# Query parts made a group ahead, own weights split before the seven-product sum, value pages requested before products, in a one-layer hybrid step

## The chip, the cores and the metric

The kernel runs on one core of a Trainium2 chip. Its measure is the device time of one execution in microseconds (us); the time of a kernel is the median of its runs. The engines that matter are TensorE (PE, with PEld for its weight loads), VectorE (DVE), ScalarE (ACT), GpSimd (POOL) and SyncE (SP); the last two also issue transfers.

## The reference: one step of a hybrid decoder

One layer takes 512 new prompt tokens and 8 x 4 sample tokens (each sample has 512 past tokens in four pages of 128 rows), 544 tokens in all, of width 1024. Everything is fp32.

```
def half_ffn(x, g_pre, g_post, w_gate, w_up, w_down):
    h = rmsnorm(x, g_pre)
    u = jax.nn.silu(h @ w_gate) * (h @ w_up)
    return x + 0.5 * rmsnorm(u @ w_down, g_post)
...
logits = jnp.einsum('bqhcd,bkhcd->bchqk', q, k, preferred_element_type=jnp.float32) * (ATT_DQ ** -0.5)
...
p = jax.nn.softmax(logits, axis=-1)
a = p[:, 0] - lam * p[:, 1]
return jnp.einsum('bhqk,bkhd->bqhd', a.astype(v.dtype), v)
```

The layer is a half FFN (inner width 2816), a token mixer, and a second half FFN. The mixer runs two groups of four heads side by side: differential attention (each head has two components of 64 dimensions with a softmax each; the second is subtracted with a factor) and an mLSTM with matrix memory. Samples attend to their cached pages of keys and values and to their own new tokens.

## The kernel before

**Precision and tiling.** Tokens lie along the free dimension in two halves of 272. TensorE multiplies in a rounded fp32 form, and precision is kept by splitting an operand into a high and a low part: `parts` casts a raw weight tile to its high part on ScalarE (L241) and subtracts that from the raw tile on VectorE for the low part (L242). A product is then three matmuls: high x high, high x low, low x high (L253 to L255 for plain products; L489 to L491 for the products of a fast scheme with seven block products, `seven`; L751 to L753 for `plain`, rows of weights that the scheme leaves out and which are called the own rows: `OWN` is 6 rows of 128).

**What sets the order.** The program is written as Python generators that take turns, and a scheduler of the framework then sets the order of the instructions on each engine, under the waits for data and for buffers. Each engine works through its own list in order. Tiles rotate through pools: "acc" and "aux" have three PSUM banks each, "smp" two; an "aux" bank (`ps_tile`) is free again when its last reader is done.

**FFN down products** (`down`, L709 to L833). At the end, four tiles of outputs (i = 0 to 3) are made from the third block product of the scheme: the weights are split (`parted(sums, i)`), `seven` runs its products, a part of the work that finishes the other half is taken (`_take(finish, ...)`: norm and the bridge into the mixer, with the sums "ssp" of squares, L320 and L351, that a product with ones at L285 adds up over the partitions), then the own weights of the tile (128x768) are split and multiplied. Both FFNs use this code.

**The mixer** (lines about 1180 to 1700). The projections of the mixer's input (L253 to L255, with weights split as they come) are interleaved with the attention of the prompt, the mLSTM and the samples, one head after another. For a head, `key_parts` makes the high and low parts of the keys ("cs", L1289 and L1290, 64x512), and `attn_block` handles one block of 128 queries. `query_parts` makes the four parts of the queries: for each component the high part twice (into the component's own 64 partitions and into the other 64, by ScalarE, L1299) and the low part twice (by VectorE, L1301): four casts and four subtractions of 64x128 a block. Their buffer is one tile "vb" of which there is one (`bufs=1`). Two pairs of products, one for a component (L1317), fill one aux bank each; VectorE adds the bias and takes the maximum (L1323, L1325: instructions named CUSTOM_DVE or ISA, that read the bank), ScalarE takes the exponential (L1328), and the parts of the next block are made after the present block's products. Transposes (L1343), the products with the values and the normalisation (L1251, L1252) follow in later turns.

**The samples** (`attn_samples`, L1355 on). Two groups of four samples. Key pages are gathered by POOL's indirect transfers (L1366, seven buffers "pgin"), three ahead, transposed (L1392), copied ("pgT", L1393) and multiplied with the queries. Then for each of four pages, four value pages (one for each sample of the group) are multiplied (L1455), and behind these the four of the next page are requested.

Of the kernel before, what the change touches and what calls it, by code (L numbers as in the profile page):

```python
# [14 lines left out]
ALU = mybir.AluOpType  # L15
# [45 lines left out]
         "q1 m21 t13 h12 d12 q0 q1 m21 t14 h13 d13 q0 q1 m21 t15 h14 d14 q1 m21 t16 h15 d15 q1 t17 h16 d16 q1 "  # L61
         "h17 d17 q1 s01")

NQ = 2
AHEAD = 3
NBK = 32
# [139 lines left out]
class _Builder:  # L206
# [502 lines left out]
    def down(self, li, ns, rows, factors, late, xd, gpost, finish):  # L709
# [30 lines left out]
        def parted(ts, i, n=KH):  # L740
            w = self.w_tiles()
            self.parts(ts[i // 2][:, 0:n, i % 2 * 128:i % 2 * 128 + 128], *(x[:, 0:n] for x in w))
            return w
# [80 lines left out]
        u = raw(2, 0, OWN, None if li else lambda j: self.ha.tile([128, OWN, 256], F32, name="ha"))  # L824
        next(finish)
        for i in range(4):
            w = parted(sums, i)
            ps = self.acc_tile(1)
            self.seven(ps, 3, w, first=True)
            _take(finish, A_STEPS * i // 3 - A_STEPS * max(0, i - 1) // 3)  # L830
            plain(ps, parted(u, i, OWN), 1, 0, OWN, False, True)
            self.post_evac(ps, i, 1, gpost, False, add=True)
        next(finish)  # L833

# [454 lines left out]
            nc.scalar.copy(out=kc[own], in_=k[own, 0:SEQ])  # L1289
            nc.vector.tensor_tensor(out=kc[other], in0=k[own, 0:SEQ], in1=kc[own].bitcast(F32), op=ALU.subtract)  # L1290

    def query_parts(self, q):

        nc = self.nc
        self.qt = qt = self.pg.tile([128, 4, 128], F32R, name="vb", bufs=1)
        for c in range(2):
            own, other = self.comp(c)
            for rows in (own, other):
                nc.scalar.copy(out=qt[rows, c, :], in_=q[own])  # L1299
            for rows in (own, other):  # L1300
                nc.vector.tensor_tensor(out=qt[rows, 2 + c, :], in0=q[own], in1=qt[own, c, :].bitcast(F32),  # L1301
                                        op=ALU.subtract)

    def attn_block(self, h, qb, q, k, vt):
        nc = self.nc
# [1 line left out]
        n = (qb + 1) * 128  # L1307
        if qb == 0:
            self.key_parts(k)
            self.query_parts(q[:, 0:n])  # L1310
            yield
        P = []
        z = wk.tile([128, 6], F32, name="z", bufs=6)
        for c in range(2):
            ps = self.ps_tile()
            for a in range(2):
                nc.tensor.matmul(ps[:, 0:n], lhsT=self.qt[:, 2 * a + c, :], rhs=self.ks[c][:, 0:n],  # L1317
                                 start=a == 0, stop=a == 1)
            L = wk.tile([128, 512], F32, name="L", bufs=5)
            f = max(n - 256, 0)  # L1320
            strip = self.strip[:, h, :]
            if f:
                nc.vector.tensor_tensor_reduce(L[:, 0:f], ps[:, 0:f], strip[:, 0:1].to_broadcast([128, f]), 1.0, -3.0e38,  # L1323
                                               ALU.add, ALU.max, z[:, 4 + c:5 + c])
            nc.vector.tensor_tensor_reduce(L[:, f:n], ps[:, f:n], strip[:, 256 - n + f:256], 1.0,  # L1325
                                           z[:, 4 + c:5 + c] if f else -3.0e38, ALU.add, ALU.max, z[:, c:c + 1])
            nc.vector.tensor_scalar_mul(z[:, c:c + 1], z[:, c:c + 1], -1.0)
            nc.scalar.activation(out=L[:, 0:n], in_=L[:, 0:n], func=AF.Exp, bias=z[:, c:c + 1],  # L1328
                                 accum_out=z[:, 2 + c:3 + c])
            P.append(L)  # L1330
        self.blocks_left -= 1
        if qb < 3:
            self.query_parts(q[:, n:n + 128])
        nc.vector.reciprocal(out=z[:, 2:4], in_=z[:, 2:4])
        nc.vector.tensor_tensor(out=z[:, 3:4], in0=z[:, 3:4], in1=self.nlam, op=ALU.mult)
        nc.vector.tensor_scalar(out=P[1][:, 0:n], in0=P[1][:, 0:n], scalar1=z[:, 3:4], scalar2=None, op0=ALU.mult)
# [22 lines left out]
    def attn_samples(self):  # L1359
# [14 lines left out]
        for g in range(2):  # L1374
# [74 lines left out]
            for j in range(4):  # L1449
                sj = slice(32 * j, 32 * j + 32)  # L1450
                nc.tensor.matmul(po[sj, :], lhsT=an[:, sj], rhs=vtok, start=True, stop=False, tile_position=(0, 32 * j))
            for pg in range(NPG):
                for j in range(4):
                    sj = slice(32 * j, 32 * j + 32)
                    nc.tensor.matmul(po[sj, :], lhsT=aT[:, pg * 128 + 32 * j:pg * 128 + 32 * j + 32], rhs=vps[j],  # L1455
                                     start=False, stop=pg == NPG - 1, tile_position=(0, 32 * j))
                if pg < NPG - 1:
                    vps = [page(1, 4 * g + j, pg + 1) for j in range(4)]
                if g == 0:
                    yield  # L1460
                yield
# [555 lines left out]
```

## Time and profile before

| | us |
|---|---|
| median of three runs | 1106.17 |
| the runs | 1103.99, 1106.17, 1108.48 |
| profiled execution, its own time | 1102.31 |
| span of its profile | 1100.4 |
| TensorE busy / weight loads busy | 1085.4 / 1048.0 |
| VectorE busy / ScalarE busy / POOL busy | 854.4 / 640.4 / 162.8 |

A row of a timeline or of the waits names the line of the program, the engine, the operation and its output and inputs by the program's names. Brackets at a row's end say how long the engine was idle before it, and who ended that. A matmul's record is longer than the distance to the next one's start, because matmuls are pipelined; the distance from start to start is what a matmul costs in a full row. Fused steps of attention (the bias with the maximum) show two rows on VectorE: the operation and a short read of its accumulator.

### The profile page before, as it was taken

How to read it: one execution, taken by the hardware profiler on the slowest of the kernel's cores; microseconds unless marked ns; L12 is line 12 of the kernel's file. 1: busy time of each engine (PE TensorE's matmuls, PEld its weight loads, DVE VectorE, ACT ScalarE, POOL GpSimd, SP SyncE). 2: the span in 40 equal slices, each digit the busy share in tenths (PEclk: the TensorE clock that was granted, in tenths of full speed). 3: DMA queues.
4: the chain of work that ended last, by engine and by line, in shares of the span. 5: the costliest groups of instructions: out<-in, count | busy, mean ns of one | idle time of the engine just before them, and what ended most of it. 6: DMA issues, size and time to landing. Idle time of an engine off the chain costs nothing. (4 is left out here: it accounts for less than half of the span.)

```text
span 1100.4 us, 21550 instructions
## 1 busy us (share of the span) xinstructions
PE 1085.4 (99%) x8610; PEld 1048.0 (95%) x8610; DVE 854.4 (78%) x1630; ACT 640.4 (58%) x1292; POOL 162.8 (15%) x212
## 2 busy tenths in 40 slices
PE   9999999999999999999999999999999999999997
PEld 8999999999999999899889879999999999999997
DVE  5898787887677899658686578799987788957764
ACT  6554554565557757666564557675554455555664
POOL 3100000001110324420244441001000000012000
PEclk9999999999999999999999999999999999999999
DMA  9723233236995245633355646764233323299722
GB/s 265 255 94 116 78 116 115 78 97 188 228 225 170 65 143 155 200 111 87 96 160 172 190 143 189 235 220 135 89 116 94 99 82 102 71 276 208 187 98 82
DMA packets 145620, 160.33 MB, mean 146 GB/s; under 512 B 6045, under 2 KB 135429, under 8 KB 144240
## 3 DMA queue, kind: packets, MB, share of 16 engines
q1 hardware_dynamic: 115040, 99.05, 29.6%
q0 software_dynamic: 27472, 57.14, 21.0%
q10 hardware_dynamic: 3008, 2.78, 0.9%
q8 instruction: 67, 1.10, 0.4%
q14 instruction: 33, 0.27, 0.1%
HBM read 143.19 MB, written 16.28 MB: 145 GB/s over the span
## 5 line engine op out<-in xcount | busy, mean ns | idle before, releaser
L241 ACT CAST wh<-raw 128x512 fp32r<-128x512 f32 (+2 forms) x165 | 127.1, 794 | 98.5 <-PE acc L254 30.3
L242 DVE TENSOR_TENSOR wl<-raw,wh 128x512 fp32r<-128x512 f32 (+2 forms) x165 | 147.2, 904 | 43.2 <-ACT wh L241 42.8
L253 PE MATMUL acc<-h,wh 128*128 128x272 f32 x552 | 164.6, 298 | 0.0
L255 PE MATMUL acc<-h,wl 128*128 128x272 f32 x552 | 160.5, 291 | 0.1
L254 PE MATMUL acc<-h,wh 128*128 128x272 f32 x552 | 159.7, 290 | 0.0
L491 PE MATMUL acc<-t,wl 128*128 128x272 f32 x472 | 136.8, 290 | 0.0
L489 PE MATMUL acc<-t,wh 128*128 128x272 f32 x472 | 136.8, 290 | 0.0
L490 PE MATMUL acc<-t,wh 128*128 128x272 f32 x472 | 136.2, 289 | 0.0
L253 PEld LDWEIGHTS acc<-h,wh 128*128 128x128 f32 x552 | 104.0, 188 | 7.8 <-issue 7.3
L255 PEld LDWEIGHTS acc<-h,wl 128*128 128x128 f32 x552 | 103.8, 188 | 0.9 <-issue 0.6
L254 PEld LDWEIGHTS acc<-h,wh 128*128 128x128 f32 x552 | 104.1, 189 | 0.2
L489 PE MATMUL acc<-h,wh 128*128 128x272 f32 x360 | 104.2, 290 | 0.0
L491 PE MATMUL acc<-h,wl 128*128 128x272 f32 x360 | 104.2, 289 | 0.0
L490 PE MATMUL acc<-h,wh 128*128 128x272 f32 x360 | 103.6, 288 | 0.0
L242 DVE TENSOR_TENSOR wl<-X,wh 128x1024 fp32r<-128x1024 f32 x66 | 80.7, 1223 | 29.4 <-ACT wh L241 29.3
L241 ACT CAST wh<-X 128x1024 fp32r<-128x1024 f32 x66 | 69.3, 1050 | 40.2 <-PE aux L490 25.8
L490 PEld LDWEIGHTS acc<-t,wh 128*128 128x128 f32 x472 | 89.0, 189 | 0.0
L491 PEld LDWEIGHTS acc<-t,wl 128*128 128x128 f32 x472 | 88.8, 188 | 0.2 <-DVE wl L242 0.2
L489 PEld LDWEIGHTS acc<-t,wh 128*128 128x128 f32 x472 | 88.8, 188 | 0.0
L738 POOL DMA_DIRECT2D late<-in_ffn_w_down_dram x12 | 18.8, 1563 | 436.6 <-DMA late<-in_ffn_w_down_dram 197.4
L491 PE MATMUL aux<-h,wl 128*128 128x272 f32 x240 | 69.4, 289 | 0.0
L489 PE MATMUL aux<-h,wh 128*128 128x272 f32 x240 | 69.4, 289 | 0.0
(522 smaller groups left out, 3290.3 us busy)
## 6 DMA issues: line engine op xcount, KB each, us to landing
raw<-in_ffn_w_gate_dram SPq DMA_DIRECT2D x18, 1024.0 KB, 5.4
raw<-in_w_in_dram SPq DMA_DIRECT2D x28, 512.0 KB, 4.3
late<-in_ffn_w_down_dram POOLq DMA_DIRECT2D x12, 1024.0 KB, 10.7
rawx<-in_ffn_w_up_dram SPq DMA_DIRECT2D x10, 1024.0 KB, 5.4
X<-in_ffn_w_up_dram SPq DMA_DIRECT2D x8, 1024.0 KB, 5.4
raw<-in_ffn_w_down_dram SPq DMA_DIRECT2D x8, 1024.0 KB, 9.6
raw<-in_ffn_w_down_dram SPq DMA_DIRECT2D x10, 768.0 KB, 4.6
raw<-in_w_out_dram SPq DMA_DIRECT2D x7, 1024.0 KB, 5.4
```

The lines of the kernel that those rows point to most:

```text
L241: self.nc.scalar.copy(out=high, in_=src)
L242: self.nc.vector.tensor_tensor(out=low, in0=src, in1=high.bitcast(F32), op=ALU.subtract)
L253: nc.tensor.matmul(ps, lhsT=wh, rhs=xh(k0 + k), start=st, stop=False)
L254: nc.tensor.matmul(ps, lhsT=wh, rhs=xl(k0 + k), start=False, stop=False)
L255: self.last_mm = nc.tensor.matmul(ps, lhsT=wl, rhs=xh(k0 + k), start=False, stop=sp).ins
L489: nc.tensor.matmul(ps, lhsT=wh[:, k, cs], rhs=high, start=st, stop=False, skip_group_check=True)
L490: nc.tensor.matmul(ps, lhsT=wh[:, k, cs], rhs=low, start=False, stop=False, skip_group_check=True)
L491: self.last_mm = nc.tensor.matmul(ps, lhsT=wl[:, k, cs], rhs=high, start=False, stop=sp, skip_group_check=True).ins
L738: nc.gpsimd.dma_start(out=ts[j], in_=rows_of(a, j, up), accum_op=ALU.add)
```

## The change

It has three parts.

- In the last loop of `down` the own weights are split together with the tile's other weights, ahead of `seven`, not behind it.
- Query parts are no longer made for each block of 128. A table of twelve groups says which blocks of which head go together, one or two blocks wide (128 or 256 queries). The first group is made with the first key parts, and each further one when the block that starts the group before it has had its score products. Groups with an even number use the one tile "vb", groups with an odd number four tiles "sqe" (four buffers of 128x272 that other stages use too). A group is thus made ahead of the head in which it is used.
- For sample group one (the second), three of the next four value pages are requested before the products with the present four, the fourth behind them.

```
-            w = parted(sums, i)
+            w, own = parted(sums, i), parted(u, i, OWN)
             ps = self.acc_tile(1)
             self.seven(ps, 3, w, first=True)
             _take(finish, A_STEPS * i // 3 - A_STEPS * max(0, i - 1) // 3)
-            plain(ps, parted(u, i, OWN), 1, 0, OWN, False, True)
+            plain(ps, own, 1, 0, OWN, False, True)
...
+QUERIES = ((0, 0, 1), (0, 1, 3), (0, 3, 4), (1, 0, 2), (1, 2, 3), (1, 3, 4),
+           (2, 0, 1), (2, 1, 3), (2, 3, 4), (3, 0, 2), (3, 2, 3), (3, 3, 4))
...
-    def query_parts(self, q):
-        self.qt = qt = self.pg.tile([128, 4, 128], F32R, name="vb", bufs=1)
+    def query_parts(self, i):
+        if i == len(QUERIES):
+            return
+        h, first, end = QUERIES[i]
+        n = 128 * (end - first)
+        q = self.X[:, 4 + h, 128 * first:128 * end]
+        if i % 2:
+            qt = [self.tmp.tile([128, HA], F32R, name="sqe", bufs=4)[:, 0:n] for _ in range(4)]
+        else:
+            t = self.pg.tile([128, 4, 128], F32R, name="vb", bufs=1)
+            qt = [t[:, j, :] for j in range(4)]
...
+        for qb in range(first, end):
+            self.qt[h, qb] = [x[:, 128 * (qb - first):128 * (qb - first) + 128] for x in qt]
...
-            self.query_parts(q[:, 0:n])
+            if h == 0:
+                self.qt = {}
+                self.query_parts(0)
...
-                nc.tensor.matmul(ps[:, 0:n], lhsT=self.qt[:, 2 * a + c, :], rhs=self.ks[c][:, 0:n],
+                nc.tensor.matmul(ps[:, 0:n], lhsT=self.qt[h, qb][2 * a + c], rhs=self.ks[c][:, 0:n],
...
-        if qb < 3:
-            self.query_parts(q[:, n:n + 128])
+        for i, (head, first, _) in enumerate(QUERIES):
+            if (head, first) == (h, qb):
+                self.query_parts(i + 1)
...
+                early = [page(1, 4 * g + j, pg + 1) for j in range(3)] if g and pg < NPG - 1 else []
...
-                    vps = [page(1, 4 * g + j, pg + 1) for j in range(4)]
+                    vps = early + [page(1, 4 * g + j, pg + 1) for j in range(len(early), 4)]
```

Lines of the new program are two further on than in the old one up to the query parts, and 14 or 15 further behind them (L242 is L244, L1301 is L1312, L1317 is L1331, L1325 is L1339).

The rows below are the engines' lists, before and after. First VectorE at the end of the first FFN, where "ha" holds the own weights, "late" and "raw" other weights, h, X, ssp and sq belong to the finishing of the halves. Before:

```order
L302 SCALAR_TENSOR_TENSOR h_4221<-X_3983,gain,h_4219 128x272
L320 TENSOR_TENSOR ssp_4358<-ssp_4358,sq 128x272
L242 TENSOR_TENSOR wl<-ha,wh 128x768
L320 TENSOR_TENSOR ssp_4358<-ssp_4358,sq 128x272
L242 TENSOR_TENSOR wh<-raw_gates,wh 128x4x4 x2
L320 TENSOR_TENSOR ssp_4358<-ssp_4358,sq 128x272
L242 TENSOR_TENSOR wh<-raw_gates,wh 128x4x4 x2
L320 TENSOR_TENSOR ssp_4358<-ssp_4358,sq 128x272 x3
L344 TENSOR_TENSOR h_3000<-acc,h_3000 128x272
L320 TENSOR_TENSOR ssp_4358<-ssp_4358,sq 128x272
L351 TENSOR_TENSOR ssp_3003<-ssp_3003,sqe 128x272
```

And now:

```order
L244 TENSOR_TENSOR wl<-late_3014,wh 128x1024
L244 TENSOR_TENSOR wl<-ha,wh 128x768
L371 TENSOR_TENSOR h_2999<-h_2999,rpost 128x544
L346 TENSOR_TENSOR h_3000<-acc,h_3000 128x272
L372 TENSOR_TENSOR X_3983<-X_3983,h_2999 128x2x272
L353 TENSOR_TENSOR ssp_3003<-ssp_3003,sqe 128x272
L304 SCALAR_TENSOR_TENSOR h_4225<-X_3983,gain,h_4223 128x272 x4
L322 TENSOR_TENSOR ssp_4362<-ssp_4362,sq 128x272
L244 TENSOR_TENSOR wh<-raw_gates,wh 128x4x4 x2
L322 TENSOR_TENSOR ssp_4362<-ssp_4362,sq 128x272
```

The last subtraction for own weights now stands right behind that of the tile's other weights, ahead of the steps of the bridge (L371, L372, L304) that stood in front of it.

Second, TensorE at the first two blocks of head 0 (a row of 128x128 is a product of block 0, one of 128x256 of block 1; acc rows are projections). Before:

```order
L1317 MATMUL aux<-cs,vb 128x128 x4
L253 MATMUL acc<-h_4218,wh 128x272
L254 MATMUL acc<-h_4220,wh 128x272
L255 MATMUL acc<-h_4218,wl 128x272
L253 MATMUL acc<-h_4218,wh 128x272
L254 MATMUL acc<-h_4220,wh 128x272
L255 MATMUL acc<-h_4218,wl 128x272
L253 MATMUL acc<-h_4218,wh 128x272
L1317 MATMUL aux<-cs,vb 128x256
L254 MATMUL acc<-h_4220,wh 128x272
```

And now:

```order
L1331 MATMUL aux<-cs,vb 128x128 x4
L1331 MATMUL aux<-cs,sqe 128x256 x2
L255 MATMUL acc<-h_4222,wh 128x272
L256 MATMUL acc<-h_4224,wh 128x272
L257 MATMUL acc<-h_4222,wl 128x272
L1331 MATMUL aux<-cs,sqe 128x256 x2
```

The products of block 1 stand right behind those of block 0, with three projections between its two pairs; at heads 1 and 3 the eight products of the two blocks stand in one row.

Third, VectorE at block 0 of head 2, around the read of the first component's bank (the first L1325 of 128x128). Before:

```order
L1290 TENSOR_TENSOR cs<-k,cs 64x512
L1327 TENSOR_SCALAR z<-z 128x1
L1301 TENSOR_TENSOR vb<-X_3983,vb 64x128 x4
L1230 TENSOR_TENSOR v<-acc,r 128x272
L1334 RECIPROCAL z<-z 128x2
L1325 ISA L,z<-aux,strip 128x128
```

And now:

```order
L1292 TENSOR_TENSOR cs<-k,cs 64x512
L1341 TENSOR_SCALAR z<-z 128x1
L1232 TENSOR_TENSOR v<-acc,r 128x272
L1312 TENSOR_TENSOR sqe<-X_3983,sqe 64x256
L1339 ISA L,z<-aux,strip 128x128
```

The four subtractions for this block have gone further ahead, and one of the next group, 256 queries wide, stands in front of the read.

On POOL and on TensorE the requests and the products of the value pages stand in the same rows before and after.

More of the change, by code (lines that the diff above doesn't have):

```diff
@@ L1298, in query_parts @@
             for rows in (own, other):
-                nc.scalar.copy(out=qt[rows, c, :], in_=q[own])
+                nc.scalar.copy(out=qt[c][rows], in_=q[own])
             for rows in (own, other):
-                nc.vector.tensor_tensor(out=qt[rows, 2 + c, :], in0=q[own], in1=qt[own, c, :].bitcast(F32),
-                                        op=ALU.subtract)
+                nc.vector.tensor_tensor(out=qt[2 + c][rows], in0=q[own], in1=qt[c][own].bitcast(F32), op=ALU.subtract)
+        for qb in range(first, end):
+            self.qt[h, qb] = [x[:, 128 * (qb - first):128 * (qb - first) + 128] for x in qt]
     def attn_block(self, h, qb, q, k, vt):
```

## The prediction

> **What bounds the kernel now.** I read the page's busy line first, then the stretches of 100 us, then the waits of TensorE and of its weight loader, and last the timelines around the waits that the change aims at.
>
> ```profile
> span 1100.4 us, 21550 instructions
> PE 1085.4 (99%) x8610; PEld 1048.0 (95%) x8610; DVE 854.4 (78%) x1630; ACT 640.4 (58%) x1292; POOL 162.8 (15%) x212
> 300.00:400.00 100.00, 98.79 (x771) 97.32 (x770) 83.62 (x136) 66.41 (x116) 18.50 (x30) 1.00 0.63 154
> 400.00:500.00 100.00, 96.98 (x769) 90.56 (x768) 76.88 (x285) 62.66 (x176) 34.42 (x42) 1.00 0.52 147
> 500.00:600.00 100.00, 98.11 (x822) 88.47 (x821) 74.73 (x278) 59.44 (x192) 29.61 (x37) 1.00 0.45 127
> ```
>
> TensorE is the bound: 15 us of the span are not busy, and the windows (length, then PE, loader, VectorE, ScalarE, POOL, clock, DMA share, GB/s) say that the three in which the edits stand hold 1.2, 3.0 and 1.9 us of that. No instruction of TensorE is removed, so the change can only take waits away. The views of its waits say how many there are to take:
>
> ```profile
> PE aux L1317 <- ACT vb L1299: 1.4, 2, 0.9
> PE acc L753 <- DVE wl L242: 0.7, 1, 0.7
> PE aux L1317 <- DVE vb L1301: 0.7, 1, 0.7
> PEld aux L1317 <- ACT vb L1299: 2.5, 5, 1.1
> PEld aux L1317 <- DVE vb L1301: 1.6, 4, 0.9
> PEld acc L753 <- DVE wl L242: 0.9, 1, 0.9
> PEld smp L1455 <- DMA pgin<-in_cache_v_dram,idx: 1.2, 1, 1.2
> ```
>
> (Total us, times, longest.) The first three are matmuls, the last four weight loads. The three edits aim at just these three lines, L1317, L753 and L1455. Summed, the matmul rows give 2.8 us and the loader rows 6.2 us. The truth lies between: a matmul's record lasts longer than the gap to the next one's start, so idle time is partly hidden in it, while a loader's wait holds slack that the matmuls ahead of it cover. **6.2 us, 0.56% of the time, is the ceiling of the whole change**; nothing else is offered by it.
>
> The Trainium skill ("Perfetto Trace Analysis", Identifying the Most-Contended Engine) says that matmul occupancy misleads, since pipelined matmuls look other than they are, and that weight-load busy time is to be used. By that rule 52 us of this span would be idle on the loader (1100.4 less 1048.0) where the matmul row shows 15. The trace agrees so far that the loader's waits are the longer ones, but by either measure these three places hold what was summed above.
>
> **The change, part by part.** I price each stall by starts: a 272-column matmul starts 0.125 us after the one ahead when nothing is late (377.58 to 377.70 below).
>
> *The own weights' split in FFN0's down loop.*
>
> ```profile
> 377.58 0.28 PE L751 MATMUL acc<-u,wh 128*128 128x272 f32 x1
> 377.70 0.28 PE L752 MATMUL acc<-u,wh 128*128 128x272 f32 x1
> 378.71 0.39 PE L753 MATMUL acc<-u,wl 128*128 128x272 f32 x1 [0.72 <-DVE wl L242]
> 382.82 0.39 PE L285 MATMUL aux<-ssp,ones 128*128 128x272 f32 x1
> 377.71 0.95 DVE L242 TENSOR_TENSOR wl<-ha,wh 128x768 fp32r<-128x768 f32 x1
> 382.02 0.44 DVE L351 TENSOR_TENSOR ssp<-ssp,sqe 128x272 f32<-128x272 f32 x1 [0.15 <-ACT sqe L349]
> ```
>
> The low part of the last own weights is made at 377.71 to 378.66, and the matmul that loads it starts at 378.71 instead of 377.83: 0.88 us are lost. In the new order this subtraction (0.95 us) and that of the round before stand ahead of VectorE's work for the bridge into the mixer, so it is some 3 us early and the 0.88 go. What is late next is that work: VectorE is busy without a gap here, so the two subtractions push the sums behind them to where they would have ended anyway, and the sums do not come sooner. Their reader is L285. With 0.88 taken off it could start at 381.94; the last sum ends at 382.46 today, and in the new order can end earlier by its own idle 0.15 and by a part of the 0.43 that another sum takes, since the evacuation in front of it comes sooner with TensorE. I take 382.2 for L285, so **0.6 us gained**, bounds 0 (the sum ends where it did) and 0.88; a further sum of 0.43 that lands behind makes the low end -0.3. In FFN1's down loop, the same code, the new order on VectorE and ScalarE has the same rows in the same places: 0.
>
> *Query parts, head 0.* The old kernel makes parts of 128 queries at a time into one buffer, so the parts of block 1 can only be written once block 0's products have read it.
>
> ```profile
> 426.32 0.34 PE L253 MATMUL acc<-h,wh 128*128 128x272 f32 x1
> 427.12 0.29 PE L253 MATMUL acc<-h,wh 128*128 128x272 f32 x1
> 428.29 0.39 PE L1317 MATMUL aux<-cs,vb 128*128 128x256 f32 x1 [0.88 <-ACT vb L1299]
> 428.52 0.29 PE L254 MATMUL acc<-h,wh 128*128 128x272 f32 x1
> 427.09 0.28 DVE L1325 CUSTOM_DVE_ANT_0 L<-aux,strip 128x128 f32<-128x128 f32 x1
> ```
>
> 1.17 us lie between 427.12 and 428.29, so 1.04 are lost. Now those parts are in buffers of their own, made before block 0's. But the products of both blocks then stand almost in a row, and each pair fills one of the three banks of "aux": block 0's two pairs, block 1's first, and block 1's second must wait until VectorE has read the bank of block 0's first (L1325, to 427.37). TensorE reaches it at 426.32 + 2 x 0.23 (428.29 to 428.52) + 3 x 0.125 = 427.16, so 0.2 are lost there, 0.35 if VectorE, which now makes these four subtractions of 64x256 ahead of that read, is 0.1 late and the signal costs something. So **0.7 us gained**, bounds -0.9 (all four subtractions delay the read in full, worked out in the second rival) and 1.04.
>
> *Head 1.*
>
> ```profile
> 459.93 0.62 PE L1392 MATMUL smp<-base,pgin 128*128 128x128 f32 x4
> 460.52 0.29 PE L254 MATMUL acc<-h,wh 128*128 128x272 f32 x1
> 461.33 0.39 PE L1317 MATMUL aux<-cs,vb 128*128 128x256 f32 x1 [0.52 <-ACT vb L1299]
> 460.16 0.28 DVE L1325 CUSTOM_DVE_ANT_0 L<-aux,strip 128x128 f32<-128x128 f32 x1
> PEld smp L1392 <- ACT pgT L1393: 1.5, 4, 0.6
> ```
>
> 0.81 between starts, 0.68 lost. Now eight products stand in a row, four of them before 459.93; the last pair is reached at 459.93 + 0.46 = 460.39 and its bank is free at 460.45: 0.1 lost in place of 0.68. Behind them the page transposes (L1392) come later against the products that cover their copies; the loader's waits for these copies between 420 and 480 (last row) are 1.5 us in four, and I give back half of one, 0.2. **0.4 us**, bounds -0.4 and 0.7.
>
> *Head 2.*
>
> ```profile
> 491.10 0.30 PE L1317 MATMUL aux<-cs,vb 128*128 128x128 f32 x1
> 491.41 0.29 PE L254 MATMUL acc<-h,wh 128*128 128x272 f32 x1
> 492.40 0.33 PE L1317 MATMUL aux<-cs,vb 128*128 128x128 f32 x1 [0.70 <-DVE vb L1301]
> 490.98 0.69 DVE L1290 TENSOR_TENSOR cs<-k,cs 64x512 fp32r<-64x512 f32 x1
> 491.77 1.19 DVE L1301 TENSOR_TENSOR vb<-X,vb 64x128 fp32r<-64x128 f32 x4
> 493.00 0.44 DVE L1230 TENSOR_TENSOR v<-acc,r 128x272 f32<-128x272 f32 x1
> ```
>
> Here the wait is for the low parts: 0.99 between starts, 0.86 lost. The new order has these parts well ahead, so the first pair runs through at 491.1. The second pair, five products on (491.95 to 492.0), needs the bank of that first pair, and VectorE's read of it now stands behind the key parts (to 491.67), z, the value's evacuation (0.44) and one subtraction of 64x256. I estimate that one at 0.42, between 0.29 for 64x128 (1.19 / 4) and 0.69 for 64x512. That puts the read's end at 491.77 + 0.36 + 0.42 + 0.28 = 492.83 and the pair at 492.9: 0.95 lost in place of 0.86. One stall is swapped for another: **-0.1**, bounds -0.8 (ScalarE's casts for that subtraction late as well) and 0.5 (the value's evacuation comes behind).
>
> *Head 3.* Eight products in a row again, and block 1's first pair waits for a read of block 0's time:
>
> ```profile
> 538.28 0.34 DVE L1252 TENSOR_SCALAR X<-aux,hg 128x128 f32<-128x128 f32 x1
> 538.23 0.34 PE L253 MATMUL acc<-h,wh 128*128 128x272 f32 x1
> 538.79 0.29 PE L254 MATMUL acc<-h,wh 128*128 128x272 f32 x1
> 539.10 0.39 PE L1317 MATMUL aux<-cs,vb 128*128 128x256 f32 x1
> 539.45 0.29 PE L253 MATMUL acc<-h,wh 128*128 128x272 f32 x1
> 539.73 0.39 PE L1317 MATMUL aux<-cs,vb 128*128 128x256 f32 x1
> ```
>
> Before, 0.19 (538.79 to 539.10) and 0.15 (539.45 to 539.73) are lost; now the pair comes first, at 538.23, and the bank is free at 538.62: 0.4. **-0.1**, bounds -0.5 and 0.3.
>
> *What it does to the helpers.* 64 casts and 64 subtractions of 64x128 become 32 and 32 of these and 16 and 16 of 64x256, some 3 us less on each of ScalarE and VectorE; at 58% and 78% busy that is worth nothing by itself. Weight splits slide by some us behind the parts but are used later still; if that cover were gone, a subtraction 512 wide, 0.69 us like that at 490.98, would show.
>
> *The value pages.* In the orders of POOL, of SyncE and of TensorE the requests for group two and the products that they wait for stand in the same rows before and after: the scheduler had already put three requests ahead, and the seven buffers come free by the same products. So **0**; if the order hid something, the loader's 1.2 us are the most to gain and a page later by one product (0.13 us) the least to lose.
>
> The sum: 0.6 + 0.7 + 0.4 - 0.1 - 0.1 + 0 = **1.5 us** gained. The rest of the L1317 rows, at the third and fourth blocks, is too small for a term. On the profiled execution, 1102.31 us with a span of 1100.4, that makes 1100.8 and 1098.9. This execution lies 3.9 us under the median of the three runs (1103.99, 1106.17, 1108.48), so the forecast for the median is 1106.17 - 1.5 = **1104.7 us**.
>
> **The rivals.**
>
> *Everything listed is gained.* The matmuls and loads just wait no more: between 2.8 and 6.2 us, say the middle, 4.5, which gives 1101.7. For it: each row has its releaser made earlier. Against: in three of four heads a bank takes over.
>
> *Slower: the banks.* One mechanism, at the first two blocks of each head: with the parts ready, TensorE runs six to eight score products into three banks, and each further pair waits for VectorE's read of the first, queued behind the very subtractions that were moved ahead. If at heads 0 and 2 all four 64x256 subtractions (4 x 0.42 = 1.7 us) delay the read by their full length, head 0 loses 0.2 + 1.7 = 1.9 in place of 1.04, head 2 has three more of them behind its one, 0.95 + 3 x 0.42 = 2.2 in place of 0.86, and heads 1 and 3 come to their low bounds, 0.4 each: 0.9 + 1.3 + 0.8 = 3.0 us more, less 0.6 from the down loop, so +2.4 and 1108.6. It decides once head 0's first read ends later than 428.2 (427.16 + 1.04). Against it: of head 0's subtractions the order has all four ahead of the key parts, where VectorE follows the same products as before.
>
> The Trainium skill (the same page, Optimization Strategy) speaks for this rival: consistent bubbles can mean that there is not enough PSUM for the next tile, so buffers would have to come first. By it the waits at L1317 would stay as they are and only their releaser would change, which gives the down loop's 0.6 alone, 1105.6, a time that lies with the third rival's. The trace shows one such row, L1252 at head 3.
>
> *The change does not do what it says.* Pages and FFN1 do not move at all in the order; if the down loop's gain is eaten whole by L285 and heads cancel, nothing is left: 1106.2.
>
> **How the numbers follow.** The forecast gets 0.58, everything gained 0.14, the banks 0.13, nothing 0.15. The kernel's runs differ by 4.5 us among three, so I count a median good to about 2 us; what a measurement of this kernel can tell from no change is about 0.5% (5.5 us). The likeliest case alone spans 1101.9 to 1107.5 (its sum may be off by 0.8 as well); the whole range runs from 1101.7 - 1.4 below to the banks' 1108.6 above, **1100.3 to 1108.6**. Faster by over 0.5% needs less than 1100.6: a third of the case in which everything is gained, and a tenth of the forecast's and of the others, 0.12. Slower than 1111.7: a tenth of the banks, little of the rest, 0.04. Within: 0.84.
>
> **What would show it.** In the new profile no wait of L753 on the split, and L285 ending near 382.2 against it; at L1317 no wait on parts from casts but waits on VectorE's reads ("z" or "L") or on L1252, the largest at head 2, near 1 us; L1455's wait unchanged near 1.2 on the loader; windows 300 to 600 with 1 to 2 us more TensorE busy time in all. A wait on L1299 or L1301 that is left, a stall over 1.2 us at head 0, or a weight split that TensorE waits for would make the steps wrong; a time under 1100 would mean that the ceiling was read wrongly.

## The result, and the profile after

The changed kernel takes 1104.73 us (median of 22 runs, 1101.08 to 1109.71), the kernel before beside it 1107.15 us (22 runs): a ratio of 0.9979, 95% interval 0.9969 to 0.9989, which is 2.3 us faster (1.2 to 3.4). Forecast were 1104.7 us and 1.5 us gained. The interval excludes no change, but the gain is less than the 0.5% named in the prediction. Three further measurements of the same two kernels, below, gave 0.9951, 0.9957 and 0.9970, so the gain is rather 2 to 5 us, and the forecast of 1.5 us too small.

The profiled execution shows none of this at first sight: its span is longer than the one before. These are the page's lines and the waits of TensorE (total us, times, longest), and one of its loader, of the changed kernel:

```profile
span 1102.9 us, 21497 instructions
PE 1085.4 (98%) x8610; PEld 1048.1 (95%) x8610; DVE 852.2 (77%) x1614; ACT 637.7 (58%) x1276; POOL 165.5 (15%) x212
...
PE aux L1545 <- DVE X L1254: 1.8, 1, 1.8
PE acc L753 <- ACT wh L243: 1.2, 1, 1.2
PE aux L1331 <- DVE z L1339: 1.0, 2, 0.7
PE acc L755 <- DVE wl L244: 0.5, 1, 0.5
PE aux L1331 <- DVE vb L1312: 0.4, 2, 0.2
...
PEld smp L1471 <- DMA pgin<-in_cache_v_dram,idx: 1.2, 1, 1.2
```

The waits on ScalarE's query casts are gone from the score products (now L1331), and so is the wait on the own weights near 378 us: the 0.5 at L755 stands at 987 us, in the second FFN. In their place are waits on VectorE's reads of a bank ("z"). The wait on value pages (L1471) is 1.2 as before. The prediction named a wait on L1301 that is left as a sign that its steps are wrong, and such a wait is there: TensorE still waits for low parts at L1331 (L1301 is now L1312), 0.4 us in two at the first block of head 0. New are 1.8 at L1545 and 1.2 + 0.5 at L753 and L755; the experiments ask whether these belong to the change.

**The first FFN's end**, TensorE and then VectorE:

```profile
377.48 0.29 PE L754 MATMUL acc<-u,wh 128*128 128x272 f32 x1
377.61 0.29 PE L755 MATMUL acc<-u,wl 128*128 128x272 f32 x1
381.49 0.29 PE L1088 MATMUL acc<-h,wh 128*100 128x272 f32 x1
381.72 0.73 PE L287 MATMUL aux<-ssp,ones 128*128 128x272 f32 x2
373.52 0.95 DVE L244 TENSOR_TENSOR wl<-ha,wh 128x768 fp32r<-128x768 f32 x1
381.23 0.44 DVE L353 TENSOR_TENSOR ssp<-ssp,sqe 128x272 f32<-128x272 f32 x1
```

The subtraction is done by 374.47, 3 us ahead of its matmul, which starts 0.13 us after the one in front of it. The sum that L287 reads ends at 381.67, and L287 starts 0.23 us after the matmul before it: almost nothing of the 0.88 us came back there.

**Head 0 and head 2**, again TensorE and then VectorE of each:

```profile
426.19 0.29 PE L257 MATMUL acc<-h,wl 128*128 128x272 f32 x1
426.77 0.50 PE L1331 MATMUL aux<-cs,sqe 128*128 128x256 f32 x2 [0.29 <-DVE z L1339]
426.43 0.28 DVE L1339 CUSTOM_DVE_ANT_0 L<-aux,strip 128x128 f32<-128x128 f32 x1
...
490.34 0.29 PE L256 MATMUL acc<-h,wh 128*128 128x272 f32 x1
491.33 0.41 PE L1331 MATMUL aux<-cs,vb 128*128 128x128 f32 x2 [0.71 <-DVE z L1339]
490.22 0.43 DVE L1232 TENSOR_TENSOR v<-acc,r 128x272 f32<-128x272 f32 x1
490.57 0.40 DVE L1312 TENSOR_TENSOR sqe<-X,sqe 64x256 fp32r<-64x256 f32 x1
490.90 0.28 DVE L1339 CUSTOM_DVE_ANT_0 L<-aux,strip 128x128 f32<-128x128 f32 x1
```

At head 0 the last pair of block 1 starts 0.58 us after the projection ahead of it, where these shapes follow each other at 0.13 to 0.14 us when nothing is late (at 503.3 us in the same profile): 0.45 us are lost. It starts right after the read of block 0's bank has ended. At head 2 the queue in front of the read is the one that the prediction named: the value's evacuation, one subtraction of 64x256 (0.40, estimated 0.42), the read. The stall is 0.99 us between starts, 0.86 lost, as long as the one that it replaces.

The wait on low parts stands at head 0's first block, on TensorE:

```profile
424.47 0.22 PE L1331 MATMUL aux<-cs,vb 128*128 128x128 f32 x1
424.87 0.44 PE L1331 MATMUL aux<-cs,vb 128*128 128x128 f32 x2 [0.18 <-DVE vb L1312]
425.49 0.33 PE L1331 MATMUL aux<-cs,vb 128*128 128x128 f32 x1 [0.18 <-DVE vb L1312]
425.65 0.45 PE L1331 MATMUL aux<-cs,sqe 128*128 128x256 f32 x2
```

From the first product of the block to the first one behind the block pass 1.18 us, before 0.73 (425.59 to 426.32): 0.45 us are lost here, and the prediction had no term for them.

### The profile page after: what moved, and what is told of

Its sections match the earlier page's. It is cut to its first block, busy times and chain, and to the rows that moved or that the text cites. A ratio compares the mean times of both kernels' runs of the same rounds, so it can differ in the third digit from the quotient of the medians.

```text
span 1102.9 us, 21497 instructions
## 1 busy us (share of the span) xinstructions
PE 1085.4 (98%) x8610; PEld 1048.1 (95%) x8610; DVE 852.2 (77%) x1614; ACT 637.7 (58%) x1276; POOL 165.5 (15%) x212
## 5 line engine op out<-in xcount | busy, mean ns | idle before, releaser
L244 DVE TENSOR_TENSOR wl<-raw,wh 128x512 fp32r<-128x512 f32 (+2 forms) x165 | 147.0, 904 | 43.5 <-ACT wh L243 42.9
L244 DVE TENSOR_TENSOR wl<-X,wh 128x1024 fp32r<-128x1024 f32 x66 | 80.8, 1224 | 30.6 <-ACT wh L243 30.6
```

Of the source, the lines that this page charges most:

```text
L244: self.nc.vector.tensor_tensor(out=low, in0=src, in1=high.bitcast(F32), op=ALU.subtract)
```

## The experiments

To separate what repeats from what only one execution shows, I numbered the matmuls of each profile in order of start (8610 in every kernel here) and took the start of the same number in two profiles. The table gives the change of that distance over a stretch, against the first profile of before; negative is a gain in us. "Before" are three further profiles of the old order (the kernel before twice more, and between them the run of the third part alone, whose order is the same), "changed" the four of the changed kernel. Where the two orders differ locally, the same number is not always the same product, so a stretch's end can be off by 0.1 us. From 566 us on, all engines have the same order before and after.

| stretch (matmul numbers; us in the first profile) | before | split only | queries only | changed | fourth bank (2) | parts once | singles | forecast |
|---|---|---|---|---|---|---|---|---|
| first FFN's end (2900-3253; 374-422) | 0.01, 0, 0 | -0.87 | -0.01 | -0.88, -0.87, -0.87, -0.87 | -0.88, -0.88 | -0.87 | -0.88 | -0.6 |
| head 0 (-3400; -442) | 0.36, 1.23, 0.42 | 0.33 | -0.72 | -0.74, -0.59, -0.63, -0.71 | -0.79, -0.78 | -0.82 | -0.78 | -0.7 |
| head 1 (-3600; -467) | 0, 0, 0.01 | 0 | -0.29 | 0.32, -0.28, -0.28, -0.29 | -0.28, -0.30 | -0.49 | 1.86 | -0.4 |
| head 2 (-3900; -506) | 0.02, 0, 0.01 | -0.02 | -0.03 | -0.04, -0.02, -0.02, -0.05 | -0.22, -0.19 | -0.22 | 0.24 | 0.1 |
| its last blocks (-3940; -512) | 0, 0.02, 0 | 0.01 | -0.61 | -0.61, -0.60, -0.60, -0.61 | -0.62, -0.63 | -0.60 | -0.86 | none |
| head 3 (-4200; -542) | 0.02, 0.02, 0.02 | 0.03 | -0.10 | -0.10, -0.11, -0.11, -0.09 | -0.56, -0.54 | -1.13 | -0.15 | 0.1 |
| behind it (-4250; -549) | 0, 0, 0.01 | 0.02 | -0.28 | -0.27, -0.29, -0.29, -0.29 | -0.37, -0.37 | -1.06 | 0.76 | none |

**The third part alone.** Edit: on the kernel before,

```
+                early = [page(1, 4 * g + j, pg + 1) for j in range(3)] if g and pg < NPG - 1 else []
...
+                    vps = early + [page(1, 4 * g + j, pg + 1) for j in range(len(early), 4)]
```

> The kernel before with the third part alone (three of the next four value pages of group two requested ahead of the products). Theory A (waits were exchanged at the first two parts; the third does nothing): on all five engines the instructions stand in the order of the kernel before, so the ratio is 1 within the measurement's own interval, and the profile is a second look at the kernel before: the L753 wait (0.9 on the loader) and the L1317 waits on query parts (some 4 on the loader) are back, the wait at L1455 stays near 1.2. Any single wait of 1 us or more that this profile has and the first does not is then a matter of one execution. Theory C (the earlier requests carry part of the gain): 0.5 to 1.2 us faster, the wait at L1455 gone.

Measured: 1105.18 against 1105.43 us, 0.9997 (0.9984 to 1.0011). The order of all engines is that of before. This third part does nothing to the order; the run is a second profile of the kernel before. Three places of this profile are slower than in the first: 1.23 us at head 0, 1.1 us at value pages near 557 us (eight products L1456 take 2.16 us, in the first profile 1.06; the loader's waits for value pages add up to 2.2 us here and to 0.2 to 1.5 in every other profile), and 2.6 us near 987 us. At head 0 the query casts stand behind casts of weights, for whose transfer ScalarE waits 0.75 us here and 0.45 in the first, so that TensorE loses 1.34 us where it lost 1.04. That is 0.3 us of the 1.23. The other 0.9 us comes from the granted clock (TensorE, then a window with its length, the busy times, the clock, the DMA share and GB/s):

```profile
428.86 0.39 PE L1317 MATMUL aux<-cs,vb 128*128 128x256 f32 x1 [1.19 <-ACT vb L1299]
429.49 0.43 PE L253 MATMUL acc<-h,wh 128*128 128x272 f32 x1
429.71 0.43 PE L254 MATMUL acc<-h,wh 128*128 128x272 f32 x1
430.00:431.00 1.00, 1.00 (x6) 1.00 (x6) 1.00 (x5) 0.47 (x2) 0.01 (x1) 0.50 0.75 234
```

Right behind the stall the clock is 0.50 from 429.13 to 432.54 us, and projections start 0.225 us apart in place of 0.125.

**The first part alone.** Edit: the two lines of `down` as in the change.

> The kernel before with the first part alone (own weights split ahead of the seven products). Theory A: the 0.88 us at L753 near 378 go and do not come back at the sums: the start of the head 0 scores is 0.9 us earlier than with the kernel before, the whole 0.6 to 1.0 us faster (ratio 0.9991 to 0.9994, not to be told from 1 by the time alone). Rival (the lateness moves on to the sums at L285): 0 to 0.3 us.

Measured: 1103.09 against 1105.43 us, 0.9980 (0.9964 to 0.9995). In the table 0.87 us stand, all of them at the first FFN's end, and none comes back by 422 us: theory A, as far as the sums at L285 go. But 0.33 us come back at head 0, so that 0.5 us are left by 549 us: TensorE arrives earlier there, and the query casts still stand behind a cast that waits for its weights to land (ScalarE waits 0.98 us, in the first profile of before 0.45). Two further profiles of the old order lose 0.36 and 0.42 us at that place too; against them the whole 0.87 is kept. The time's own interval (0.6 to 4.0 us) holds both.

**The second part alone.** Edit: the table and the two functions of the query parts as in the change.

> The kernel before with the second part alone (query parts a group ahead). Theory A: head 0 gains some 0.8 us, heads 1 and 2 0.1 each, head 3 nothing, so 1.0 us faster (ratio 0.9991), with waits of L1331 on VectorE's reads of 0.3 to 0.9 at heads 0, 2 and 3. Theory B (the 2.0 us at L1545 near 560 that the changed kernel's profile shows are a consequence of the new order in the attention): that wait of 1.8 to 2.0 us stands here too, in the same place, and the time is 1 us slower than before or the same.

Measured: 1102.05 against 1105.43 us, 0.9971 (0.9959 to 0.9983). The table has -2.0 us in all by 549 us, twice what theory A said: 0.72 at head 0 and 0.29 at head 1 as in the changed kernel, but also 0.61 between 506 and 512 us and 0.28 behind head 3, which I had not counted. The wait at L1545 near 560 us is not there, which speaks against theory B.

**The changed kernel again, twice more beside other runs, and the kernel before again.** No edit.

> The changed kernel once more, for a second profile. Theory A (the 2.0 us at L1545 near 560 and the 2.0 us at L753 near 985 were matters of that one execution): neither is there again, the waits at L1331 of 0.35 (head 0), 0.17 (head 1), 0.87 (head 2) and 0.39 (head 3) are, to within 0.1. Theory B (they belong to the change): both are there again. Time: 0.9969 to 0.9989 of the kernel before, as measured.

> The changed kernel beside the three above, on the same chip. By start times of the same product in the profiles (the earlier profiles give 3.1 us of gain over the first profile of before, of which 0.97 stand by 382 us, 0.87 at heads 0 and 1, 0.6 near 509 and 0.3 near 549): these steps again to within 0.15 each. By the first 22 runs 0.9979, by the second measurement 0.9951 of before: if both are one effect, 0.996 to 0.998 here. Wait of L753 near 985 on a transfer: 1.7 to 2.6 us again, as in all profiles but the first of before.

Measured: 1099.51 against 1105.43 us, 0.9951 (0.9932 to 0.9970); 1100.74 against 1104.90, 0.9957 (0.9940 to 0.9975). Both ratios lie below what was expected (0.9969 to 0.9989, and 0.996 to 0.998). The steps agree to 0.15 us between the profiles in every stretch but one: the first profile's 0.32 at head 1 is a wait on a page copy that the other three do not have. The wait at L753 near 985 us is in both, so that for this one theory A failed (it is taken up below). The wait of 1.8 us at L1545 is in neither. In the first profile it looks like this, TensorE and then VectorE:

```profile
559.30 0.37 PE L255 MATMUL acc<-h,wh 128*128 128x272 f32 x1
561.45 0.49 PE L1545 MATMUL aux<-vt,kt 128*128 128x130 f32 x2 [1.78 <-DVE X L1254]
560.70 0.44 DVE L1232 TENSOR_TENSOR q<-acc,r 128x272 f32<-128x272 f32 x1 [2.40 <-PE acc L255]
```

VectorE's evacuation waits for a product that started at 558.37 us, and begins 2.3 us after it; behind it stands the read that TensorE needs. The last profile of the kernel before has the same stall at the same instructions, by its own line numbers:

```profile
563.15 0.49 PE L1529 MATMUL aux<-vt,kt 128*128 128x130 f32 x2 [1.70 <-DVE X L1252]
562.40 0.44 DVE L1230 TENSOR_TENSOR q<-acc,r 128x272 f32<-128x272 f32 x1 [2.36 <-PE acc L253]
```

One of four profiles of each order has it, so it is not the change's. What holds the evacuation up for 2 us I could not see.

> The kernel before once more: ratio 1 within its interval. Its profile says which of the waits in the two profiles of this order are the program's and which one execution's. If the gain of the changed kernel is that of the places that three profiles of it share, the products at 382, 467, 512 and 549 us start 0.97, 1.8, 2.4 and 2.7 us later here than in them, counted from the same product at 374 us, each to within 0.2 plus any one-off wait that can be named; at 985 a wait on a transfer of between 0 and 2.6 us.

> The kernel before, for a fourth profile of its order. One thing is open: the transfer that ScalarE waits for near 985 us was late, by 1.6 to 2.6 us of TensorE's time, in all four profiles of the changed kernel and in one of three of this order. If its landing is a matter of the execution alone, it is late here in about half of the cases and nothing follows from either outcome alone; if it were late only with the changed kernel's timing, it is not late here. The steps to 549 us are those of the other profiles of this order, apart from single waits on transfers at head 0. Time: 1 of before within 0.2%, since the same order measured 0.9997 and 1.0018.

Measured: 1105.75 against 1103.88 us, 1.0018 (1.0004 to 1.0032), and 1107.00 against 1106.22, 1.0003 (0.9988 to 1.0018), for one and the same kernel. With the 0.9997 above, the ratio of equal orders scatters by 0.1 to 0.2%, a little more than its intervals say. The stretches are those of the first profile but for 0.36 and 0.42 us at head 0. The wait near 985 us stands in all four profiles of the changed kernel, and in two of the four of the old order (2.6 and 1.9 us more by matmul 7750; 0 and -0.1 in the others). In the changed kernel's first profile:

```profile
985.23 0.83 ACT L243 CAST wh<-raw 128x768 fp32r<-128x768 f32 x1 [2.91 <-DMA raw<-in_ffn_w_down_dram]
986.12 0.40 PE L753 MATMUL acc<-u,wh 128*128 128x272 f32 x1 [1.21 <-ACT wh L243]
```

A transfer of own weights lands late, ScalarE's cast waits for it, and TensorE for the cast. All five engines have the same order there before and after. The request is issued at the same place of TensorE's order (behind 7646 products) in all thirteen profiles whose traces keep it; it takes 9.7 to 10.7 us to land in the four profiles without the wait, 11.2 in "singles" (0.6 us) and 12.2 to 13.2 in eight with it. So it is the transfer that is slower, and not its request that is later. The first and the second part alone and "parts once" have the wait as well (1.6 to 2.0 us), the two profiles of the fourth bank have not. Whether the changed kernel's timing makes it late more often, four of four against two of four does not tell; it stays open, and with it about 1 us of what the change is worth over the whole kernel (an estimate: half of the 2 us that the wait costs). The new order alone does not make it late, since the old order has it too.

> The changed kernel beside them: 0.995 to 0.998 of before; the same steps to 549 us as in its other profiles, to within 0.15.

Measured: 1100.73 against 1103.88 us, 0.9970 (0.9959 to 0.9981), the same steps.

**A fourth bank.** Edit, in the changed kernel, so that the second component of blocks 0 and 1 uses a bank of "acc":

```
-            ps = self.ps_tile()
+            ps = self.acc.tile([128, 512], F32, name="acc") if c and qb < 2 else self.ps_tile()
```

> The changed kernel, with the second component's score products of blocks 0 and 1 put into an accumulation bank (pool acc) in place of aux, so that four pairs have four banks. Bank theory (what is left of the waits at the score products is VectorE's late read of one of three banks): the 0.36 at head 0's last pair, the 0.17 at head 1, the 0.85 at head 2 and the 0.39 at head 3 go, 1.5 us or more in the profile up to 545 us, and the time is 1.5 us below the changed kernel's (ratio to it 0.9986). Rival (TensorE only meets the same lateness some products later, at the next user of VectorE's results or of an acc bank): under 0.5 us, with new waits of the same size on acc banks or on transposes.

> The version with score products in accumulation banks once more. Its first profile is 0.9 us ahead of the changed kernel's by 549 us (0.5 at head 2, 0.4 at head 3, nothing at heads 0 and 1, where the lateness came back at an acc bank and at the page transposes). If that is the program's: the same 0.9 here to within 0.2, and the time 1 us below the changed kernel's, ratio to before 0.994 to 0.997. If the transposes and acc banks give it back: no more than 0.3.

Measured: 1098.74 against 1104.90 us, 0.9943 (0.9924 to 0.9962), the changed kernel beside it 0.9957; and 1098.52 against 1103.88, 0.9962 (0.9945 to 0.9978), the changed kernel 0.9970. Both profiles are 0.8 to 0.9 us ahead of the changed kernel's by 549 us, about half of the stalls that go (0.45, 0.17, 0.86 and 0.45 us at heads 0 to 3). The rest came back at the next user, as these rows of the second profile show:

```profile
426.63 0.39 PE L255 MATMUL acc<-h,wh 128*128 128x272 f32 x1 [0.22 <-DVE X L1233]
460.68 0.66 PE L1407 MATMUL smp<-base,pgin 128*128 128x128 f32 x4 [0.51 <-ACT pgT L1408]
489.57 0.44 PE L1331 MATMUL acc<-cs,vb 128*128 128x128 f32 x2 [0.22 <-DVE cs L1292]
```

At head 0 the projection behind the scores needs an acc bank that VectorE reads 0.4 us too late, at head 1 the page transposes meet their copy earlier, and at head 2 the products now wait for the second key part (0.38 us lost in place of 0.86). Only head 3 gains in full. Bank theory and rival are each right for about half of the time. By medians (2.0 and 2.2 us below the changed kernel) this is the fastest version that makes all the parts; the ratios' intervals overlap with the changed kernel's, and both its profiles lack the late transfer near 985 us, so of the 2 us only the 0.9 are shown.

**Parts made once.** Edit, in the changed kernel:

```
         h, first, end = QUERIES[i]
+        if i:
+            for qb in range(first, end):
+                self.qt[h, qb] = self.qt[0, 0]
+            return
```

> The changed kernel with the query parts made for the first group only and used for all blocks: it leaves out the other 11 groups of casts and subtractions, so its attention result is that of wrong queries; its time says what the parts cost on the path. Bank theory: the waits of 0.36 at head 0 and 0.39 at head 3 stay, since they are waits for a read that no parts delay (head 0's by 0.1), and at head 2 the wait falls by the subtraction that stood ahead of the read, from 0.85 to some 0.45: 0.5 us below the changed kernel. Rival (the parts' 13 us on VectorE and as much on ScalarE still load the path all over the attention): 1.5 us or more below it, in places spread over 425 to 550 us.

Measured: 1098.82 against 1104.90 us, 0.9929 (0.9904 to 0.9955); by the table 5.2 us by 549 us where the changed kernel beside it has 2.8. This kernel leaves out all groups but the first. So by some 2.4 us the other parts are still on the path, most of it around head 3 and behind: the rival. (Without them the scheduler's order differs too; what that alone does was not tried.) The waits on banks stay meanwhile, as the bank theory said, and at head 0 even grow:

```profile
PE aux L1335 <- DVE z L1343: 0.7, 1, 0.7
PE aux L1335 <- ACT kt L1247: 0.5, 1, 0.5
PE aux L1335 <- DVE X L1254: 0.3, 1, 0.3
```

(The waits of TensorE from 380 to 560 us; the first is at head 0, the second at head 2, the third at head 3.)

**Groups of one block.** Edit, in the changed kernel:

```
+QUERIES = tuple((h, qb, qb + 1) for h in range(4) for qb in range(4))
```

> The changed kernel with sixteen groups one block wide in place of twelve of one or two, still a group ahead and in the two kinds of buffers in turn. If being ahead is what gains and not the width: the same waits as the changed kernel's to within 0.3 us at each head, time within 0.7 us of it. If the wider instructions (16 fewer on each of two engines) matter: 1 us or more slower than it. At head 2 the subtraction ahead of the read is 0.29 and not 0.42, so that wait should be 0.1 to 0.2 shorter.

Measured: 1103.70 against 1104.90 us, 0.9987 (0.9971 to 1.0004), 3 us above the changed kernel beside it. By the table its gains, 2.7 us, are lost again at heads 1 and 2 and behind head 3 (2.9). Its largest waits, from 380 to 560 us:

```profile
PE smp L1394 <- ACT z L281: 1.6, 1, 1.6
PE aux L1330 <- ACT kt L1246: 1.0, 1, 1.0
PE smp L1406 <- ACT pgT L1407: 1.0, 2, 0.5
```

Being ahead is not enough. At 441 us the sample products wait 1.6 us for a chain on ScalarE that is short of time there, an order which the scheduler made of the sixteen groups. My two expectations were both about parts; what came was a wait elsewhere. Whether the extra instructions or only the other order cause it was not tried.

## Why the prediction was right, and where not

**TensorE as the bound, and the ceiling.** Right: the busy time is 1085.4 us in both, and the gain by 549 us (the four changed profiles are at -2.3 to -2.9 against 0 to 1.3 for the old order; the means lie 3.2 us apart, or 3.0 without the 0.9 us of the halved clock) is below 6.2. But "nothing else is offered by it" was wrong, for what stands below under "What was left out": 0.8 to 0.9 us were gained at waits that are in none of the seven rows of the ceiling.

**The own weights.** The mechanism was right, the term too small: 0.87 us in place of 0.6. The step that failed is "I take 382.2 for L285": L287 starts with hardly a wait. The sum it needs ended 0.8 us earlier than before, because the evacuation in front of it followed TensorE, and of VectorE's work behind the two subtractions nothing was pushed out.

**Head 0 and head 1.** Head 0: 0.7 forecast, 0.6 to 0.7 measured, but the agreement is luck. The stall on the bank is 0.45 where 0.35 was said. The first two blocks, however, which the term was about, gained only 0.3 to 0.4 us in the four changed profiles, since the first block's products now wait 0.45 to 0.61 us longer for their own low parts. The missing 0.3 came from the third block, which had no term: there twelve products (four of the scores, eight page transposes) took from 431.65 to 433.55 us, and now take from 430.12 to 431.70. In the old order they alternate, and the loader waits for a low part among them, a wait that no matmul row shows:

```profile
432.80 0.19 PEld L1317 LDWEIGHTS aux<-cs,vb 128*128 128x128 f32 x1 [0.19 <-DVE vb L1301]
```

Against the three other profiles of the old order the same edit is worth 0.4 to 1.2 us more at head 0, with 0.9 of the 1.2 by the halved clock. Head 1: 0.28 in place of 0.4; within the stretch 0.24 are given back by 457 us, at the page transposes (forecast 0.2), and 0.54 gained at the scores and just behind (forecast 0.58).

**Head 2 and head 3.** The swap of one stall for another of the same length at head 2 was right to 0.1 us (0.86, forecast 0.95), by the queue that was written down. At head 3 the bank cost 0.45 (0.4): the pair starts 0.55 us after the product ahead of it, and 0.10 with a fourth bank. Still the stretch gained 0.1 where 0.1 was to be lost. The Trainium skill ("Perfetto Trace Analysis", Optimization Strategy) says that a repeated bubble can mean too few PSUM buffers; at head 2 the trace agrees so far that 0.86 us on parts became 0.86 on a bank, and with a fourth bank 0.38 us of them stayed, on a key part. At head 0 it agrees for less than half (0.45 of 1.04 us), and the down loop is none of its kind.

**What was left out.** The step that failed most is "the rest of the L1317 rows, at the third and fourth blocks, is too small for a term". One such row is the 0.3 us at the third block of head 0, above. Between 506 and 512 us the old kernel has this, TensorE, then ScalarE, then VectorE:

```profile
510.25 0.59 PE L1317 MATMUL aux<-cs,vb 128*128 128x384 f32 x2 [0.61 <-DVE X L1252]
505.83 1.25 ACT L1299 CAST vb<-X 64x128 fp32r<-64x128 f32 x4
507.00 0.91 DVE L1301 TENSOR_TENSOR vb<-X,vb 64x128 fp32r<-64x128 f32 x3
508.23 0.17 DVE L1334 RECIPROCAL z<-z 128x2 f32<-128x2 f32 x1 [0.32 <-ACT L L1328]
509.76 0.34 DVE L1252 TENSOR_SCALAR X<-aux,hg 128x128 f32<-128x128 f32 x1
```

And the changed one:

```profile
507.93 0.62 PE L1331 MATMUL aux<-cs,sqe 128*128 128x384 f32 x2
505.99 0.17 DVE L1349 RECIPROCAL z<-z 128x2 f32<-128x2 f32 x1 [0.67 <-ACT L L1342]
507.53 0.34 DVE L1254 TENSOR_SCALAR X<-aux,hg 128x128 f32<-128x128 f32 x1
```

In the old order four casts on ScalarE stand ahead of the exponentials, which begin at 507.10, and VectorE, done with its subtractions at 507.91, is idle for 0.32 us until the exponentials are there. Its softmax steps, and the read L1252 that stands behind them, come late with ScalarE, so that the bank is free 0.6 us late. With the parts elsewhere the queues are done in time. The wait's name was not a query part but a read, so I passed over its row, though the parts were what made the read late. That is 0.6 us.

Further 0.2 to 0.3 us between 542 and 549, which the second part alone has as well, are of the same kind. VectorE and TensorE of the old kernel, and last VectorE of the changed one:

```profile
542.61 0.91 DVE L1301 TENSOR_TENSOR vb<-X,vb 64x128 fp32r<-64x128 f32 x3
543.55 0.69 DVE L1522 TENSOR_TENSOR L<-aux,L 128x512 f32<-128x512 f32 x1
544.30 0.49 PE L1529 MATMUL aux<-vt,kt 128*128 128x130 f32 x2 [0.17 <-DVE L L1522]
538.50 0.69 DVE L1538 TENSOR_TENSOR L<-aux,L 128x512 f32<-128x512 f32 x1 [0.48 <-PE aux L1534]
```

Three subtractions of query parts stand ahead of L1522, and TensorE waits for it. In the changed kernel this step (L1538) is done at 539.19, over 2 us ahead of the same products (541.59). 0.44 us are gained there, and 0.2 given back at the next pair of products, which waits for VectorE's L1548.

**Value pages and FFN1.** Right: zero. The order showed it.

**Sum and median.** By the stretches the change is worth some 2.8 us against the first profile of before, and 3.2 against the mean of four; forecast were 1.5. That 1104.7 was forecast and 1104.73 measured is luck: the kernel before measured 1107.15 beside it and not 1106.17, the gain was 2.4 us and not 1.5, and these two cancel; the same comparison gave 3 to 6 us on other occasions. What was right is the direction, the split's and the banks' mechanism and the size of the new stalls; the sum was too small by half, for the most part by the two steps named above. The first profile also flattered the kernel before: its span lacks the late transfer near 985 us that six of the eight profiles of the two orders have.

**The rivals.** "Everything gained" gave 2.8 to 6.2 us, and the 2.8 to 3.2 measured by 549 us touch its low edge, but not by its mechanism: banks took over at three heads as it was said, and 0.8 to 0.9 us came from places that it did not list. "Slower: the banks" did not decide: head 0's first read ended at 426.71 us, 0.4 us after TensorE came to the pair (426.32), and that rival needed more than 1.04. "Does not do what it says" was right for the third part alone.

## What to carry to other kernels

A wait's row names the last instruction, not the work that made it late: before an edit that clears a queue is priced, list the waits on everything that stands behind that work in the same queue, not just the waits on its own output. Where a stall on data is removed and the next product needs a buffer, write down the queue of the engine that frees the buffer; that gave the size of three new stalls to 0.1 us. And for effects of a few microseconds, compare the starts of the same instruction in several profiles: stretches without a single wait or a change of the clock repeat to 0.1 us where whole runs scatter by 5 and more.

## What the runs showed of the hardware

Between profiles of one order, single waits come and go at fixed places: a late transfer near 985 us (1.9 to 2.6 us in six of eight), a pause near 560 us in which VectorE and ScalarE start 2 us after the product that they wait for has run (in one of four of each order), and value pages near 557 and 665 us (up to 1.1 us).

The granted clock is the other part. In four of the fourteen profiles it stood at 0.50 for 3.4 us in the middle of the kernel, each time behind a stall of TensorE: at 429 us in the run of the third part alone, and near 985 us, behind the late transfer, in one profile of the old order, one of the changed kernel and that of "parts once". Beside the stall itself it cost 1.2 us at the first place (of which 0.3 came back by 442 us) and 1.5 at the others. The length of the stall does not decide: 1.48 us between starts at 429 us and 1.34 to 1.55 near 985 were followed by it, 1.9 near 985 in another profile of the changed kernel and 2.15 at 559 us in the first were not. What decides is not shown.

Most stretches between such places repeat to some hundredths of a microsecond. These waits and clock drops, and not a general slowness, make up most of the scatter between the profiled executions: the spans of the old order are 1100.2 to 1105.9 us, and the difference is found in four or five stretches.
